# MLP block products: hi and lo of the right operand in one matmul of 512 columns

## The chip, the cores and the metric

One core of one Trainium2 chip runs the whole kernel. The metric is the device time of one execution in microseconds (us). All five engines of the core work at once, each through its own queue in a fixed order: TensorE (PE) multiplies, VectorE (DVE) and ScalarE (ACT) do elementwise work, GpSimd (POOL) a few small operations, and the Sync engine's queue (SP) issues the loads.

## The reference

One block of a streaming encoder, 512 positions of 1024 features, in float32: a first part (input projection, gated branches, output projection), which the change leaves as it is, and then a squared-ReLU MLP with a hidden width of 4096 and a final norm.

```python
hf = rmsnorm(x, norm_ff_g[l])
z = jax.nn.relu(jnp.einsum('bsd,df->bsf', hf, w_ff1[l]))     # 1024 -> 4096
x = x + jnp.einsum('bsf,fd->bsd', z * z, w_ff2[l])            # 4096 -> 1024
return rmsnorm(x, norm_final_g)
```

## The kernel before

Features lie on the partitions, the 512 positions on the columns. To keep float32 accuracy with the faster fp32r matmul, every operand is split into a hi part (a cast, by ACT) and a lo part (operand minus hi, by DVE), `split_into` (L114), and each product is made of three matmuls, hi x hi, hi x lo and lo x hi, that add up in one PSUM bank. There are 7 banks in rotation.

The second MLP layer is made of plain units (`unit_k`, L262): for each of 8 slices of 128 features three matmuls of 512 columns (L265 to L267).

The first layer and some projections use a block scheme with seven instead of eight products. An output pair is 256 hidden features; its weights are four blocks, and what is multiplied is blocks of weights or sums of them (`a1`, `s31`, `s42`, `a22`) with halves of 256 positions or sums of those (the right operands, `right_of`, L322). `product` (L273) makes one of the seven: 4 slices with three matmuls of 256 columns each (L283 to L285). `block_pair` (L289) makes the products of a pair in the order P1, P2, E, P6, F, and puts P7 and D aside (`late`); they run among the next pair's products. Three banks serve a pair: A collects P1, P6, P7 and D, E collects E and F, P2 has its own; only the first 256 columns of each are used. After each product ACT or DVE reads the running sum out of the bank: copies by ACT (L298, L303, L305, L313), adds by DVE (L300, L308, L314).

The results go through `z_first` and `z_second` (L718, L722): max or min with zero and the factor 1/rms (R) on DVE, a square on ACT, and the split into z's hi (ACT) and lo (DVE), 128x512 each.

Weights come in loads of 1 MB with two load buffers (`raw`). `plan_pair` (L207) lists the steps that prepare a pair's weights: hi and lo of a1, a weight sum (L218), hi and lo of s31, two more sums (L222, L223), hi and lo of s42, hi and lo of a22. All lo parts and sums are DVE's. `pump` (L180) takes one step per product from that list if one of four buffers is free, so the preparation of later products stands in the same DVE and ACT queues as the reading of the banks.

The MLP runs in four passes (L844): 5, 4, 4 and 3 pairs of the first layer, each followed by eight units of the second layer on the eight z tiles made. Within each engine the final order is set by a scheduler when the program is built: it reorders instructions by its own estimate of when they can start, and may put matmuls of different products between one another. That order is fixed afterwards; on the chip an engine waits at each instruction for what it needs.

Of the kernel before, what the change touches and what calls it, by code (L numbers as in the profile page):

```python
# [12 lines left out]
ALU = mybir.AluOpType  # L13
# [23 lines left out]
def hybrid_block(ctx, tc, xT, vecs, w_v, w_main, w_pair, w_s, b_s, out_a, out_b):  # L37
# [12 lines left out]
    nc = tc.nc  # L50
# [46 lines left out]
    def slots(n, name, dtype=F32):  # L97
        return [Slot(f"{name}{k}", dtype) for k in range(n)]
# [8 lines left out]
    def temp(name, n=S):  # L107
        t = work.tile([P, S + 2], F32, tag="temp", name=name)
        return t[:, :n]

    def col(base, j):
        return vec[:, base + j : base + j + 1]

    def split_into(hi, lo, src, scale=None):  # L114

        if scale is None:
            nc.scalar.copy(hi, src)  # L117
            nc.vector.tensor_tensor(lo, src, hi.bitcast(F32), op=ALU.subtract)  # L118
# [55 lines left out]
    def release(o):  # L174
        if o["n"] == 2:
            wfree.append(o["buf"])
        else:
            a22_busy[0] = False

    def pump(n=1):  # L180

        while steps and n:
            step, o = steps[0]
            if o is not None and (not wfree if o["n"] == 2 else a22_busy[0]):
                return
# [50 lines left out]
    late = []  # L236

    def run_late():
        if late:
            late.pop(0)()  # L240
# [7 lines left out]
    def unit_matmuls(psum, act_hi, act_lo):  # L248

        o = units[state["next"]]  # L250
        state["next"] += 1
        for k in range(KT):
            if k == 0 or k == KT // 2:
                pump()
                need(o)
            unit_k(psum, o, k, act_hi, act_lo)
            if k == KT // 2 - 1:
                run_late()
        release(o)
        run_late()  # L260
# [9 lines left out]
    LEFT = {"P1": ("a1", 1, "B11"), "P2": ("a1", 0, "B21"), "D": ("a22", 0, "T4"), "F": ("s42", 0, "B22"),  # L270
            "P6": ("s42", 1, "T2"), "E": ("s31", 1, "T1"), "P7": ("s31", 0, "T3")}

    def product(p, right, name, out, first):  # L273

        t, g, r = LEFT[name]
        o = pairs[p][t]
        pump()
        need(o)
        for sl in range(KS):
            c = slice(sl * P, (sl + 1) * P)  # L280
            w_hi, w_lo = o["hi"][:, g, c], o["lo"][:, g, c]
            x_hi, x_lo = right[r, sl, 0], right[r, sl, 1]
            nc.tensor.matmul(out, w_hi, x_hi, start=first and sl == 0, stop=False, skip_group_check=True)  # L283
            nc.tensor.matmul(out, w_hi, x_lo, start=False, stop=False, skip_group_check=True)  # L284
            nc.tensor.matmul(out, w_lo, x_hi, start=False, stop=sl == KS - 1, skip_group_check=True)  # L285
        if name in ("P2", "D", "F", "P7"):
            release(o)

    def block_pair(p, right, first, second):  # L289

        A, P2, E = (bank()[:, :N2] for _ in range(3))
        c1, c2 = temp("c1"), temp("c2")
        product(p, right, "P1", A, True)
        nc.scalar.copy(c1[:, :N2], A)  # L298
        product(p, right, "P2", P2, True)
        nc.vector.tensor_add(c1[:, :N2], P2, c1[:, :N2])  # L300
        run_late()
        product(p, right, "E", E, True)
        nc.scalar.copy(c2[:, N2:], E)  # L303
        product(p, right, "P6", A, False)
        nc.scalar.copy(c1[:, N2:], A)  # L305
        run_late()
        product(p, right, "F", E, False)
        nc.vector.tensor_add(c1[:, N2:], E, c1[:, N2:])  # L308
        first(c1)

        def p7():
            product(p, right, "P7", A, False)
            nc.scalar.copy(c2[:, :N2], A)  # L313
            nc.vector.tensor_add(c2[:, N2:], c2[:, :N2], c2[:, N2:])  # L314

        def dd():
            product(p, right, "D", A, False)
            second(A, c2)

        late.extend([p7, dd])  # L320

    def right_of(b11, b2, t1, t2):  # L322

        r = {}
        for sl in range(KS):
            for hl in range(2):
                r["B11", sl, hl] = b11(sl, hl)
                for ss, two in ((b2, ("B21", "B22")), (t1, ("T1", "T3")), (t2, ("T2", "T4"))):
                    for e in range(2):
                        r[two[e], sl, hl] = ss[sl].t[:, hl, e * N2 : (e + 1) * N2]  # L330
        return r

    def combos(t1, t2, xa, xb):

        B11, B12, B21, B22 = xa[:, :N2], xa[:, N2:], xb[:, :N2], xb[:, N2:]
        a, b = temp("T1T3"), temp("T2T4")
        nc.vector.tensor_sub(a[:, :N2], B11, B12)
        nc.vector.tensor_sub(a[:, N2:], B22, B12)
        nc.vector.scalar_tensor_tensor(b[:, :N2], a[:, :N2], -1.0, B22, op0=ALU.mult, op1=ALU.subtract)
        nc.vector.scalar_tensor_tensor(b[:, N2:], b[:, :N2], -1.0, B21, op0=ALU.mult, op1=ALU.subtract)  # L340
        split_into(t1.t[:, 0, :], t1.t[:, 1, :], a)
        split_into(t2.t[:, 0, :], t2.t[:, 1, :], b)
# [11 lines left out]
    def rstd_of(acc, lo=0, n=NB):  # L354

        st = ps1.tile([P, S], F32, name="st")
        for b in range(n):
            nc.tensor.matmul(  # L358
                st[:, b : b + 1], acc[:, lo + b * P : lo + (b + 1) * P], inv_d, start=True, stop=True
            )  # L360
        return rstd_cols(st[:, :n])
# [32 lines left out]
    n_win = len(pairs)  # L394
# [8 lines left out]
    x_s = slots(KT, "x", F32R)  # L403
# [45 lines left out]
    xc1, xc2 = [], []  # L449
# [10 lines left out]
    r = None  # L460
# [3 lines left out]
    for i in range(2 * KT):  # L464
# [4 lines left out]
        if i == KT:  # L469
            r = rstd_of(acc)  # L470
# [4 lines left out]
        for ws, xs in ((vh, xh), (vl, xh), (vh, xl)):  # L475
            for b in range(NB):
                nc.tensor.matmul(  # L477
                    vbanks[h][b], xs[k][:, b * P : (b + 1) * P], ws,
                    start=k == 0 and ws is vh and xs is xh, stop=k == KT - 1 and xs is xl,
# [62 lines left out]
    for j in range(KT):  # L542
# [6 lines left out]
            mix(j - LAG)  # L549

    right_x = right_of(
        lambda sl, hl: x_s[sl].t[:, hl, :N2], x_s[KS:], xc1, xc2
    )

    def gate(p, n, j0, then):
# [124 lines left out]
    fb11 = slots(KS // 2, "fb11", F32R)  # L680
# [1 line left out]
    ft1 = slots(KS, "ft1", F32R)  # L682
    ft2 = slots(KS, "ft2", F32R)

    def f_b11(sl, hl):
        return fb11[sl // 2].t[:, hl, (sl % 2) * N2 : (sl % 2 + 1) * N2]

    right_f = right_of(f_b11, fb2, ft1, ft2)
    xg = {}
    for n in range(KT):  # L690
        j = n // 2 + KS * (n % 2)
        po = bank()
        unit_matmuls(po, mh, ml)
        nc.vector.tensor_add(res[j], po, res[j])
        xg[j] = temp("xg")
        nc.scalar.activation(xg[j], res[j], AF.Copy, scale=col(V_GFF, j))
        if n % 2:
            split_into(fb2[j - KS].t[:, 0, :], fb2[j - KS].t[:, 1, :], xg[j])
            combos(ft1[j - KS], ft2[j - KS], xg.pop(j - KS), xg.pop(j))
        else:  # L700
            split_into(f_b11(j, 0), f_b11(j, 1), xg[j][:, :N2])
        sum_squares(acc, res[j], n)
    give(*m_s)

# [2 lines left out]
    Rf = small.tile([P, S], F32, name="R")  # L707
# [6 lines left out]
    def z_split(i, t):  # L714
        nc.scalar.activation(t, t, AF.Square)
        split_into(*z_tile(i), t)

    def z_first(i, c1):  # L718
        nc.vector.scalar_tensor_tensor(c1, c1, 0.0, Rf, op0=ALU.max, op1=ALU.mult)
        z_split(i, c1)  # L720

    def z_second(i, n21, c2):  # L722

        nc.vector.scalar_tensor_tensor(c2[:, :N2], n21, 0.0, Rf[:, :N2], op0=ALU.min, op1=ALU.mult)
        nc.vector.scalar_tensor_tensor(c2[:, N2:], c2[:, N2:], 0.0, Rf[:, N2:], op0=ALU.min, op1=ALU.mult)
        z_split(i, c2)

    def scale_g(j, cs):
# [75 lines left out]
    def ff1_pair(p):  # L804
        def first(c1):
            if p == 0:
                wait_rf.append(lambda: z_first(0, c1))
            else:
                z_first(2 * p, c1)

        def second(n21, c2):
            z_second(2 * p + 1, n21, c2)

        block_pair(n_win + p, right_f, first, second)
        if p == 0:
            r2.append(rstd_of(acc))

            def p7_and_rf(p7=late.pop(0)):
                p7()
                nc.vector.tensor_copy(Rf, spread(r2[0]))  # L820
                wait_rf.pop()()
            late.insert(0, p7_and_rf)
# [112 lines left out]
```

## Time and profile before

| what | us |
|---|---|
| median of 3 runs | 788.54 |
| the profiled execution | 788.42 |
| its span in the trace | 786.6 |
| PE busy in it | 778.4 |
| DVE busy | 568.8 |
| ACT busy | 365.7 |

A span is the time from the first to the last instruction of the trace. Busy is the time in which an engine works on at least one instruction; matmuls overlap, so that a busy PE says nothing on how closely they follow one another. In a timeline each row has a start and a duration; the distance of two starts is what one instruction costs an engine that is never idle. "<-" behind an idle time names what ended it. The trace puts the output projection ahead of 440 us, the first pass's block products at 440 to 496, and the second layer's units behind each pass.

### The profile page before, as it was taken

What the parts mean: (1) busy time and instruction counts of PE and PEld (TensorE: products, weight loads), DVE (VectorE), ACT (ScalarE), POOL (GpSimd) and SP (SyncE); (2) the same over time, 40 slices, a digit from 0 to 9 for tenths busy, and PEclk for the clock granted to TensorE, in tenths of its full rate; (3) what the DMA queues carried; (4) which work ended last, traced back from release to release, by engine and by line L of the source; (5) the groups of instructions that cost most, each with busy time, mean ns of one, the idle gap of its engine ahead of it and who ended that gap; (6) DMA issues with size and microseconds to landing.
All of it is one profiled execution on the core that took longest, in us unless ns stands there. A gap on an engine that the chain in (4) does not pass through costs nothing.

```text
span 786.6 us, 11560 instructions
## 1 busy us (share of the span) xinstructions
PE 778.4 (99%) x4798; PEld 701.3 (89%) x4798; DVE 568.8 (72%) x854; ACT 365.7 (46%) x548; POOL 6.3 (1%) x14
## 2 busy tenths in 40 slices
PE   9999999999999999999999999999999999999996
PEld 6888899999999999999988999889988999889886
DVE  7849785566889889766769998647955687557644
ACT  8625363444344444444555676324742365226521
POOL 0000000000000000000000000000000000000000
PEclk9999999999999999999999999999999999999998
DMA  9602113331332314332633033330353024311403
GB/s 333 218 40 92 68 55 107 107 107 55 107 115 102 107 62 154 107 108 86 229 114 107 1 107 125 144 107 1 107 182 140 1 91 177 107 54 55 161 1 107
DMA packets 21443, 83.60 MB, mean 106 GB/s; under 512 B 1936, under 2 KB 2960, under 8 KB 17296
## 3 DMA queue, kind: packets, MB, share of 16 engines
q1 hardware_dynamic: 20384, 81.27, 29.5%
q10 hardware_dynamic: 1008, 1.61, 0.6%
q8 instruction: 37, 0.61, 0.3%
q14 instruction: 14, 0.11, 0.0%
HBM read 80.78 MB, written 2.10 MB: 105 GB/s over the span
## 4 chain that ended last, share of the span: by engine, by line
PE 98%; DMA 0%; ACT 0%; DVE 0%; POOLq 0%; DVEq 0%; issue 0%
PE bank L265 17%; PE bank L266 17%; PE bank L267 17%; PE bank L284 14%; PE bank L285 14%; PE bank L283 14%; PE bank L477 6%; PE bank L528 1%; DMA vec<-vecs 0%; PE bank L369 0%; PE st L358 0%; PE bank L747 0%; PE st L793 0%; DVE ob L759 0%; POOLq L929 0%; ACT x L120 0%
## 5 line engine op out<-in xcount | busy, mean ns | idle before, releaser
L117 ACT CAST whi<-raw 128x1024 fp32r<-128x1024 f32 (+1 forms) x136 | 129.0, 950 | 180.4 <-PE bank L266 117.7
L118 DVE TENSOR_TENSOR wlo<-raw,whi 128x1024 fp32r<-128x1024 f32 (+1 forms) x136 | 148.8, 1096 | 18.2 <-ACT whi L117 16.3
L117 ACT CAST whi<-wsum 128x1024 fp32r<-128x1024 f32 x64 | 67.2, 1051 | 80.9 <-PE bank L266 41.3
L265 PE MATMUL bank<-z,whi 128*128 128x512 f32 (+1 forms) x272 | 102.7, 378 | 0.0
L266 PE MATMUL bank<-z,whi 128*128 128x512 f32 (+1 forms) x272 | 102.6, 377 | 0.0
L267 PE MATMUL bank<-z,wlo 128*128 128x512 f32 (+1 forms) x272 | 102.4, 376 | 0.0
L118 DVE TENSOR_TENSOR wlo<-wsum,whi 128x1024 fp32r<-128x1024 f32 x64 | 78.2, 1222 | 21.0 <-ACT whi L117 20.2
L283 PE MATMUL bank<-ft,whi 128*128 128x256 f32 x256 | 72.5, 283 | 0.0
L285 PE MATMUL bank<-xc,wlo 128*128 128x256 f32 x256 | 72.4, 283 | 0.0
L284 PE MATMUL bank<-xc,whi 128*128 128x256 f32 x256 | 72.4, 283 | 0.0
L285 PE MATMUL bank<-ft,wlo 128*128 128x256 f32 x256 | 72.4, 283 | 0.0
L284 PE MATMUL bank<-ft,whi 128*128 128x256 f32 x256 | 72.4, 283 | 0.0
L283 PE MATMUL bank<-xc,whi 128*128 128x256 f32 x256 | 72.3, 282 | 0.0
L860 DVE TENSOR_TENSOR res<-bank,res 128x512 f32<-128x512 f32 x30 | 20.7, 691 | 60.9 <-PE bank L267 60.9
L267 PEld LDWEIGHTS bank<-z,wlo 128*128 128x128 f32 x272 | 51.2, 188 | 9.4
L265 PEld LDWEIGHTS bank<-z,whi 128*128 128x128 f32 x272 | 51.2, 188 | 9.2
L266 PEld LDWEIGHTS bank<-z,whi 128*128 128x128 f32 x272 | 51.2, 188 | 8.9
L284 PE MATMUL bank<-fb,whi 128*128 128x256 f32 x192 | 54.4, 283 | 0.0
L283 PE MATMUL bank<-fb,whi 128*128 128x256 f32 x192 | 54.4, 283 | 0.0
L283 PE MATMUL bank<-x,whi 128*128 128x256 f32 x192 | 54.4, 283 | 0.0
L285 PE MATMUL bank<-x,wlo 128*128 128x256 f32 x192 | 54.3, 283 | 0.0
L284 PE MATMUL bank<-x,whi 128*128 128x256 f32 x192 | 54.3, 283 | 0.0
(157 smaller groups left out, 1797.6 us busy)
## 6 DMA issues: line engine op xcount, KB each, us to landing
raw<-w_main SPq DMA_DIRECT2D x36, 1024.0 KB, 4.9
raw<-w_pair SPq DMA_DIRECT2D x32, 1024.0 KB, 4.8
vraw<-w_v SPq DMA_DIRECT2D x16, 256.0 KB, 5.5
xin<-xT SPq DMA_DIRECT2D x8, 256.0 KB, 5.2
res<-xT SPq DMA_DIRECT2D x8, 256.0 KB, 4.7
out_a<-o SPq DMA_DIRECT2D x4, 256.0 KB, 2.3
wsT<-w_sT ACTq DMA_DIRECT2D x2, 256.0 KB, 4.8
bsb<-b_sb ACTq DMA_DIRECT2D x2, 256.0 KB, 6.0
```

Source lines behind the costliest of these rows:

```text
L117: nc.scalar.copy(hi, src)
L118: nc.vector.tensor_tensor(lo, src, hi.bitcast(F32), op=ALU.subtract)
L265: nc.tensor.matmul(psum, hi[:, c], act_hi[k][:, cols], start=k == 0, stop=False)
L266: nc.tensor.matmul(psum, hi[:, c], act_lo[k][:, cols], start=False, stop=False)
L267: nc.tensor.matmul(psum, lo[:, c], act_hi[k][:, cols], start=False, stop=k == KT - 1)
L283: nc.tensor.matmul(out, w_hi, x_hi, start=first and sl == 0, stop=False, skip_group_check=True)
L284: nc.tensor.matmul(out, w_hi, x_lo, start=False, stop=False, skip_group_check=True)
L285: nc.tensor.matmul(out, w_lo, x_hi, start=False, stop=sl == KS - 1, skip_group_check=True)
L477: nc.tensor.matmul(vbanks[h][b], xs[k][:, b * P : (b + 1) * P], ws, start=k == 0 and ws is vh and xs is xh, stop=k == KT - 1 and xs is xl,)
L528: nc.tensor.matmul(pm[:, b * P : (b + 1) * P], vt[b][g // 4][:, (g % 4) * P : (g % 4 + 1) * P], wsT[:, g, :], start=True, stop=True,)
L860: nc.vector.tensor_add(res[j], py, res[j])
```

## The change

In the MLP's first layer (16 pairs) a slice's first two matmuls, hi x hi and hi x lo, become one: the right operand's hi and lo, two runs of 256 columns, are read as one moving operand of 512 columns and land in the two halves of the bank. The third, lo x hi, still adds 256 columns to the first half. The halves are added when the bank is read: the copies and adds take all 512 columns, and a further add on DVE (`fold`) sums the halves. For D, ACT copies the second half and DVE adds it to the first. `z_second` gets its result in one piece. The block products of the first part keep their form. The file's later lines move: `product` is at L273 in both, its matmuls at L291 (512) and L295 (256), and the new function's at L333.

```diff
+    def product(p, right, name, out, first, wide=False):
+        half, two = out[:, :N2], out.rearrange("p (e n) -> p e n", e=2)
...
+            x2 = right[r, sl]
+            x_hi, x_lo = x2[:, 0, :], x2[:, 1, :]
+            if wide:
+                nc.tensor.matmul(two, w_hi, x2, start=first and sl == 0, stop=False, **kw)
+            else:
+                nc.tensor.matmul(half, w_hi, x_hi, start=first and sl == 0, stop=False, **kw)
+                nc.tensor.matmul(half, w_hi, x_lo, start=False, stop=False, **kw)
+            nc.tensor.matmul(half, w_lo, x_hi, start=False, stop=sl == KS - 1, **kw)
...
+    def wide_pair(p, right, first, second):
+        A, P2, E = (bank() for _ in range(3))
+        c1, c2 = temp("c1"), temp("c2")
+        t1, t2, t3 = temp("t1"), temp("t2"), temp("t3")
+        def fold(out, t):
+            nc.vector.tensor_add(out, t[:, :N2], t[:, N2:])
+        product(p, right, "P1", A, True, wide=True)
+        nc.scalar.copy(t1, A)
+        product(p, right, "P2", P2, True, wide=True)
+        nc.vector.tensor_add(t1, P2, t1)
+        fold(c1[:, :N2], t1)
+        run_late()
+        product(p, right, "E", E, True, wide=True)
+        nc.scalar.copy(t2, E)
+        product(p, right, "P6", A, False, wide=True)
+        nc.scalar.copy(t3, A)
+        run_late()
+        product(p, right, "F", E, False, wide=True)
+        nc.vector.tensor_add(t3, E, t3)
+        fold(c1[:, N2:], t3)
+        first(c1)
+        def p7():
+            product(p, right, "P7", A, False, wide=True)
+            t4 = temp("t4")
+            nc.scalar.copy(t4, A)
+            nc.vector.tensor_add(t2, t4, t2)
+            fold(c2[:, N2:], t2)
+        def dd():
+            product(p, right, "D", A, False, wide=True)
+            t5 = temp("t5", N2)
+            nc.scalar.copy(t5, A[:, N2:])
+            nc.vector.tensor_add(c2[:, :N2], A[:, :N2], t5)
+            second(c2)
...
-        nc.vector.scalar_tensor_tensor(c2[:, :N2], n21, 0.0, Rf[:, :N2], op0=ALU.min, op1=ALU.mult)
-        nc.vector.scalar_tensor_tensor(c2[:, N2:], c2[:, N2:], 0.0, Rf[:, N2:], op0=ALU.min, op1=ALU.mult)
+        nc.vector.scalar_tensor_tensor(c2, c2, 0.0, Rf, op0=ALU.min, op1=ALU.mult)
...
-        block_pair(n_win + p, right_f, first, second)
+        wide_pair(n_win + p, right_f, first, second)
```

The scheduler's order on DVE, first pass, around the add of the fourth pair's P2. Before (c1_4473 is that pair's first result, wlo_4542 the lo of its s42, wlo_4604 and wlo_4635 the lo of the fifth pair's a1 and s31):

```order
L118 TENSOR_TENSOR wlo_4542<-wsum1_104,whi_4541 128x1024
L300 TENSOR_TENSOR c1_4473<-bank_4471,c1_4473 128x256
L118 TENSOR_TENSOR z4_4118<-c1_4347,z4_4118 128x512
L314 TENSOR_TENSOR c2_4348<-c2_4348 128x256
L725 SCALAR_TENSOR_TENSOR c2_4348<-c2_4348,R_4113 128x256
L218 TENSOR_TENSOR wsum0_103<-raw_4475 128x1024
L118 TENSOR_TENSOR wlo_4604<-raw_4475,whi_4603 128x1024
L222 TENSOR_TENSOR wsum1_104<-wsum0_103,raw_4475 128x512
L118 TENSOR_TENSOR wlo_4635<-wsum0_103,whi_4634 128x1024
```

After (t1_4422 is the sum that the fourth pair's P2 goes into, wlo_4479 the lo of its s42, wlo_4535 the lo of the fifth pair's a1):

```order
L345 TENSOR_TENSOR t1_4422<-bank_4418,t1_4422 128x512
...
L340 TENSOR_TENSOR c1_4420<-t1_4422 128x256
L222 TENSOR_TENSOR wsum1_104<-wsum0_103,raw_4318 128x512
L118 TENSOR_TENSOR wlo_4535<-raw_4425,whi_4534 128x1024
L118 TENSOR_TENSOR z4_4118<-c1_4313,z4_4118 128x512
L362 TENSOR_TENSOR t2_4316<-t4_4463,t2_4316 128x512
L223 TENSOR_TENSOR wsum1_104<-wsum1_104,raw_4318 128x512
L340 TENSOR_TENSOR c2_4314<-t2_4316 128x256
L118 TENSOR_TENSOR wlo_4507<-raw_4318,whi_4506 128x512
L218 TENSOR_TENSOR wsum0_103<-raw_4425 128x1024
L118 TENSOR_TENSOR wlo_4479<-wsum1_104,whi_4478 128x1024
```

The lo of s42, which P6 and F of the same pair need, has moved from just ahead of the add to twelve rows behind it, and the row of P2 is followed by a fold further down.

PE's order at the fourth pair's P6. Before (bank_4470 is the pair's A, whi_4541 and wlo_4542 its s42):

```order
L283 MATMUL bank_4470<-ft20_3762,whi_4541 128x256
L284 MATMUL bank_4470<-ft20_3762,whi_4541 128x256
L285 MATMUL bank_4470<-ft20_3762,wlo_4542 128x256
L283 MATMUL bank_4470<-ft21_3763,whi_4541 128x256
L284 MATMUL bank_4470<-ft21_3763,whi_4541 128x256
```

After (bank_4417 is A, bank_4419 is E, whi_4478 and wlo_4479 the pair's s42; bank_4526 is the fifth pair's E bank, whi_4558 the hi of its s31):

```order
L291 MATMUL bank_4417<-ft20_3762,whi_4478 128x512
L291 MATMUL bank_4419<-fb20_3754,whi_4478 128x512
L291 MATMUL bank_4526<-ft10_3758,whi_4558 128x512
L295 MATMUL bank_4417<-ft20_3762,wlo_4479 128x256
L291 MATMUL bank_4417<-ft21_3763,whi_4478 128x512
L295 MATMUL bank_4417<-ft21_3763,wlo_4479 128x256
```

Three products now begin with one wide matmul each, among them the fifth pair's E, before the first matmul that needs s42's lo.

## Rows read from the trace of the kernel before

**Rows 1.** The page's part 1: busy us, share of the span, instructions, by engine.

```profile
PE 778.4 (99%) x4798; PEld 701.3 (89%) x4798; DVE 568.8 (72%) x854; ACT 365.7 (46%) x548; POOL 6.3 (1%) x14
```

**Rows 2.** The page's part 4: shares of the span in the chain that ended last.

```profile
PE 98%; DMA 0%; ACT 0%; DVE 0%; POOLq 0%; DVEq 0%; issue 0%
```

**Rows 3.** Timeline of PE, block products: start us, us, engine, line, operation, tiles.

```profile
455.18 0.28 PE L285 MATMUL bank<-ft,wlo 128*128 128x256 f32 x1
...
456.98 0.28 PE L285 MATMUL bank<-fb,wlo 128*128 128x256 f32 x1
```

**Rows 4.** Timeline of PE, second-layer units, same columns.

```profile
510.00 0.39 PE L265 MATMUL bank<-z,whi 128*128 128x512 f32 x1
...
514.99 0.39 PE L266 MATMUL bank<-z,whi 128*128 128x512 f32 x1
```

**Rows 5.** Stretches: length, then busy us (instructions) per engine, granted clock, DMA share, GB/s.

```profile
430.00:440.00 10.00, 10.00 (x54) 8.63 (x53) 9.86 (x17) 5.82 (x9) 0.00 (x0) 1.00 0.00 0
440.00:450.00 10.00, 10.00 (x85) 9.98 (x85) 9.03 (x18) 6.20 (x11) 1.91 (x1) 1.00 0.01 2
450.00:460.00 10.00, 10.00 (x87) 10.00 (x86) 9.81 (x17) 7.28 (x14) 0.00 (x0) 1.00 0.13 37
500.00:510.00 10.00, 10.00 (x45) 8.26 (x44) 4.95 (x6) 2.73 (x3) 0.00 (x0) 1.00 0.28 105
620.00:630.00 10.00, 10.00 (x86) 10.00 (x85) 7.64 (x10) 6.02 (x9) 0.00 (x0) 1.00 0.01 2
640.00:650.00 10.00, 10.00 (x86) 10.00 (x85) 9.31 (x15) 7.33 (x12) 0.00 (x0) 1.00 0.30 105
780.00:790.00 10.00, 0.14 (x2) 0.00 (x0) 1.47 (x3) 1.27 (x2) 0.69 (x1) 0.68 0.29 105
```

**Rows 6.** Timeline of DVE, one pair of the first MLP pass.

```profile
470.17 1.23 DVE L118 TENSOR_TENSOR wlo<-wsum,whi 128x1024 fp32r<-128x1024 f32 x1 [0.18 <-ACT whi L117]
471.31 0.42 DVE L300 TENSOR_TENSOR c<-bank,c 128x256 f32<-128x256 f32 x1
471.65 0.68 DVE L118 TENSOR_TENSOR z<-c,z 128x512 fp32r<-128x512 f32 x1
472.25 0.42 DVE L314 TENSOR_TENSOR c<-c 128x256 f32<-128x256 f32 x1
472.70 0.42 DVE L725 SCALAR_TENSOR_TENSOR c<-c,R 128x256 f32<-128x256 f32 x1
...
480.25 1.23 DVE L118 TENSOR_TENSOR wlo<-wsum,whi 128x1024 fp32r<-128x1024 f32 x1
```

**Rows 7.** Groups by line and form: xcount | busy us, mean ns | idle before.

```profile
L860 DVE TENSOR_TENSOR res<-bank,res 128x512 f32<-128x512 f32 x30 | 20.7, 691 | 60.9 <-PE bank L267 60.9
...
L298 ACT COPY c<-bank 128x256 f32<-128x256 f32 x32 | 11.9, 371 | 13.5 <-PE bank L285 13.3
...
L440 ACT ACTIVATE vt<-bank,r 128x512 f32<-128x512 f32 x8 | 4.9, 689 | 10.8 <-PE bank L477 9.5 <-POOL r L351 1.4
```

**Rows 8.** Timeline, start and end of the first MLP pass's block products (PE and DVE).

```profile
443.65 0.36 PE L283 MATMUL bank<-fb,whi 128*128 128x256 f32 x1
...
443.81 0.42 DVE L300 TENSOR_TENSOR c<-bank,c 128x256 f32<-128x256 f32 x1
...
495.58 0.28 PE L285 MATMUL bank<-ft,wlo 128*128 128x256 f32 x1
495.70 0.40 PE L265 MATMUL bank<-z,whi 128*128 128x512 f32 x1
```

**Rows 9.** Timeline of ACT, first MLP pass: square, cast, hi part, copy.

```profile
459.11 0.63 ACT L715 ACTIVATE c<-c 128x512 f32<-128x512 f32 x1
459.78 0.62 ACT L117 CAST z<-c 128x512 fp32r<-128x512 f32 x1
...
462.45 1.05 ACT L117 CAST whi<-raw 128x1024 fp32r<-128x1024 f32 x1 [0.46 <-DMA raw<-w_pair]
463.40 0.37 ACT L303 COPY c<-bank 128x256 f32<-128x256 f32 x1
```

More of the change, by code (lines that the diff above doesn't have):

```diff
@@ L271, in hybrid_block @@
             "P6": ("s42", 1, "T2"), "E": ("s31", 1, "T1"), "P7": ("s31", 0, "T3")}
-    def product(p, right, name, out, first):
+    def product(p, right, name, out, first, wide=False):
+        half, two = out[:, :N2], out.rearrange("p (e n) -> p e n", e=2)
         t, g, r = LEFT[name]
@@ L281, in product @@
             w_hi, w_lo = o["hi"][:, g, c], o["lo"][:, g, c]
[L282 to L285, printed above, removed]
+            x2 = right[r, sl]
+            x_hi, x_lo = x2[:, 0, :], x2[:, 1, :]
+            kw = dict(skip_group_check=True)
+            if wide:
[4 more added lines that the diff above has]
+            nc.tensor.matmul(half, w_lo, x_hi, start=False, stop=sl == KS - 1, **kw)
         if name in ("P2", "D", "F", "P7"):
@@ L289, in block_pair @@
     def block_pair(p, right, first, second):
-        A, P2, E = (bank()[:, :N2] for _ in range(3))
+        A, P2, E = (bank() for _ in range(3))
+        A_, P2_, E_ = (b[:, :N2] for b in (A, P2, E))
         c1, c2 = temp("c1"), temp("c2")
         product(p, right, "P1", A, True)
-        nc.scalar.copy(c1[:, :N2], A)
+        nc.scalar.copy(c1[:, :N2], A_)
         product(p, right, "P2", P2, True)
-        nc.vector.tensor_add(c1[:, :N2], P2, c1[:, :N2])
+        nc.vector.tensor_add(c1[:, :N2], P2_, c1[:, :N2])
         run_late()
         product(p, right, "E", E, True)
-        nc.scalar.copy(c2[:, N2:], E)
+        nc.scalar.copy(c2[:, N2:], E_)
         product(p, right, "P6", A, False)
-        nc.scalar.copy(c1[:, N2:], A)
+        nc.scalar.copy(c1[:, N2:], A_)
         run_late()
         product(p, right, "F", E, False)
-        nc.vector.tensor_add(c1[:, N2:], E, c1[:, N2:])
+        nc.vector.tensor_add(c1[:, N2:], E_, c1[:, N2:])
         first(c1)
@@ L312, in p7 @@
             product(p, right, "P7", A, False)
-            nc.scalar.copy(c2[:, :N2], A)
+            nc.scalar.copy(c2[:, :N2], A_)
             nc.vector.tensor_add(c2[:, N2:], c2[:, :N2], c2[:, N2:])
@@ L317, in dd @@
             product(p, right, "D", A, False)
-            second(A, c2)
+            second(A_, c2)
+        late.extend([p7, dd])
+    def wide_pair(p, right, first, second):
+        A, P2, E = (bank() for _ in range(3))
+        c1, c2 = temp("c1"), temp("c2")
[29 more added lines that the diff above has]
+            second(c2)
         late.extend([p7, dd])
@@ L325, in right_of @@
         for sl in range(KS):
[L326 to L330, printed above, removed]
+            r["B11", sl] = b11(sl)
+            for ss, two in ((b2, ("B21", "B22")), (t1, ("T1", "T3")), (t2, ("T2", "T4"))):
+                for e in range(2):
+                    r[two[e], sl] = ss[sl].t[:, :, e * N2 : (e + 1) * N2]
         return r
@@ L551, in hybrid_block @@
     right_x = right_of(
-        lambda sl, hl: x_s[sl].t[:, hl, :N2], x_s[KS:], xc1, xc2
+        lambda sl: x_s[sl].t[:, :, :N2], x_s[KS:], xc1, xc2
     )
@@ L683, in hybrid_block, with f_b11 @@
     ft2 = slots(KS, "ft2", F32R)
-    def f_b11(sl, hl):
-        return fb11[sl // 2].t[:, hl, (sl % 2) * N2 : (sl % 2 + 1) * N2]
+    def f_b11(sl):
+        return fb11[sl // 2].t[:, :, (sl % 2) * N2 : (sl % 2 + 1) * N2]
     right_f = right_of(f_b11, fb2, ft1, ft2)
@@ L700, in hybrid_block @@
         else:
-            split_into(f_b11(j, 0), f_b11(j, 1), xg[j][:, :N2])
+            split_into(f_b11(j)[:, 0, :], f_b11(j)[:, 1, :], xg[j][:, :N2])
         sum_squares(acc, res[j], n)
@@ L720, in z_first, with z_second @@
         z_split(i, c1)
-    def z_second(i, n21, c2):
-        nc.vector.scalar_tensor_tensor(c2[:, :N2], n21, 0.0, Rf[:, :N2], op0=ALU.min, op1=ALU.mult)
-        nc.vector.scalar_tensor_tensor(c2[:, N2:], c2[:, N2:], 0.0, Rf[:, N2:], op0=ALU.min, op1=ALU.mult)
+    def z_second(i, c2):
+        nc.vector.scalar_tensor_tensor(c2, c2, 0.0, Rf, op0=ALU.min, op1=ALU.mult)
         z_split(i, c2)
@@ L809, in first, with second @@
                 z_first(2 * p, c1)
-        def second(n21, c2):
-            z_second(2 * p + 1, n21, c2)
-        block_pair(n_win + p, right_f, first, second)
+        def second(c2):
+            z_second(2 * p + 1, c2)
+        wide_pair(n_win + p, right_f, first, second)
         if p == 0:
```

## The prediction

> **What bounds the kernel now.** I read the busy shares first: TensorE (PE) is busy 778.4 us, 99% of the span of 786.6, VectorE (DVE) 568.8, 72% [rows 1]. The chain that ended last is 98% PE, with next to nothing given to a wait [rows 2]. So TensorE's own stream of matmuls sets the time, and only what shortens that stream or makes it wait can move it. "Busy" does not say how dense the stream is, so I took start-to-start distances from the timeline. In the block products 256 columns come every 0.120 us (15 steps from 455.18 to 456.98) [rows 3]; in the plain units 512 columns come every 0.2268 us (22 steps from 510.00 to 514.99) [rows 4]. Two matmuls of 256 thus take 0.240, one of 512 takes 0.227: a matmul has some 13 ns that do not depend on its columns, and that is all a merged pair gives back. The granted clock is 1.00 in the stretches shown up to 650, so these are figures at 2.4 GHz [rows 5].
>
> Then the stretches of 10 us show who stands second [rows 5]. In the first MLP pass DVE is busy 9.03 to 9.81 us of each 10 while the block products run; in later passes' products 7.64 to 9.31; in the second-layer units (500 to 510) only 4.95. ScalarE (ACT) is at 6.0 to 7.3. The reader should see that DVE has almost no room exactly where the change gives it more work.
>
> **What the change removes.** 16 MLP pairs x 7 products x 4 slices = 448 slices, each with one matmul less: 448 x (2 x 0.120 - 0.2268) = 5.9 us of PE. PE per pair falls from 28 x 0.36 = 10.08 to 28 x 0.3468 = 9.71 us. The weight load that goes with the removed matmul is off the path: a load overlaps the matmul ahead of it: PE goes on at the same steps in the units, where loads are busy 8.26 of 10 us, as in products, where they are busy 10.00 [rows 5].
>
> No row shows a matmul whose moving operand is two runs of 256 columns. The bounds: as one run, 0.2268 [rows 4]; as two matmuls, 0.240 [rows 3]. I take 0.2268, since columns and output bank are those of rows 4; the other end costs the whole 5.9 us.
>
> The Trainium skill, "TensorE: Matmul & The Clock Gate", section "Back-to-back issue gap", gives a gap of N/2.4 + 2.5 ns, and speaks against the change: by it a merged pair saves 2.5 ns, all of them 1.1 us. The trace has 120 and 227 ns where that gives 109 and 216, so the measurement decides.
>
> **What it adds on DVE.** Starts behind one another in the timeline: 128x1024 takes 1.14 (470.17 to 471.31), 128x256 0.34 (471.31 to 471.65), 128x512 0.60 (471.65 to 472.25); one that needs the row ahead of it 0.45 rather than 0.34 (472.25 to 472.70) [rows 6]. An add that reads a bank is no dearer: of 512 it lasts 691 ns, as the others in the timeline (0.68 to 0.69) [rows 6, 7]. Before, a pair has 4 of 1024 (three lo splits and one weight sum), 6 of 512 and 5 of 256: 9.86 us, and the trace repeats after 10.08 (470.17 to 480.25) [rows 6]. After, the adds of P2, F and P7 are 512 wide, there are three folds and D's add of 256, and the two half mins are one of 512: 4, 10 and 4, or 11.92 us. That is 2.06 us more, up to 2.4 with the dependent neighbours; 33 to 38 us for 16 pairs.
>
> **What it adds on ACT.** Four copies per pair grow from 256 columns (371 ns) to 512 (at most the 689 ns of the GELU that reads a bank), and one copy of 256 is new: at most 4 x 0.32 + 0.37 = 1.65 us per pair, and by a SBUF cast of 512 (620 ns) 4 x 0.25 + 0.37 = 1.4 [rows 7, 9]. ACT has that room, 2.7 us or more in 10 [rows 5]; it counts only where DVE or PE waits for it.
>
> So per pair DVE needs 12.0 to 12.3 us against PE's 9.7, a deficit of about 2.5. It falls on PE only when the operands' lo parts, which stand in the same DVE queue, come late. Bounds: nothing, if the lead in prepared weights holds (-5.9 us in all); everything (38 - 5.9 = +32 us). I narrow this by walking the two orders with those durations.
>
> **First pass (5 pairs).** DVE has no lead here: it comes from the output projection busy 9.86 of 10 us [rows 5]. DVE's order is unchanged up to the add of the first P2, at 443.81 [rows 8], so I start there, with PE at the product that it resumes at 443.65 [rows 8]. A product is 4 x 0.3468 = 1.39 us, one without its first matmul 1.16.
> 1. The spread of 1/rms. The last of its four scales now stands on DVE behind s42's lo of pair two. ACT can begin the hi parts ahead of it when P2 of pair two has let a buffer go, at 448.7; it makes two (0.95 each, start to next start [rows 9], and handing over) until 450.9, DVE adds 1.14 for the lo, 0.35 for a fold and 0.25 for the scale: 452.75. PE has 37 matmuls (6.4), one product and the small matmuls (0.6) until 452.05. Wait 0.8 us.
> 2. Pair four's a1. DVE's next 15 rows (2 of 1024, 10 of 512, 3 of 256: 9.3, and 0.3 for dependent neighbours) end at 462.3; behind them ACT has a square (0.67), a cast (some 0.55) and then a1's hi of 0.95 to 1.05 [rows 9]: 464.65. PE, seven products (9.7) on from 452.85, is there at 462.55. Wait 2.1.
> 3. s31's hi and s42's lo in the next group of products: 0.5.
> 4. In the before order s42's lo stands ahead of P2's add; now it stands 12 rows behind, and the first matmul of E waits for s31's hi, which waits for the weight sum on DVE. For pair five's E PE is there at 479.5; the sum is done at 480.4, the hi at 481.5. Wait 2.0.
> 5. s42's lo of pair five at 488.65, PE at 487.75: 0.9.
>
> The waits are 6.3 us. From 488.65 PE still has four products, 22 matmuls of 512 (5.0) and the rest of a product: the fifth D ends at 500.4, and two of its second-layer matmuls (0.45) are ones that before stood behind the fifth D. Without them that is 499.9 against 495.70 [rows 8]: +4.2 us, the waits less the saving.
>
> **Passes two to four (4, 4 and 3 pairs).** In the units ahead of them DVE is half idle [rows 5], so each begins with a pair's weights split ahead. The same walk over four pairs gives DVE 37.6 us for its rows up to the last s42, and PE waits of 0.2 (E's bank, still being copied) and 1.8 us (first second-layer unit's lo), against 1.5 saved: +0.5 each. With three pairs some 1.0 against 1.1: -0.1. The backlog left over drains in the units that follow, where DVE needs under 6 of 10 us.
>
> **Sum.** 4.2 + 0.5 + 0.5 - 0.1 = +5.1 us. The profiled execution took 788.42 with a span of 786.6; 788.42 + 5.1 = 793.5. The median of the runs is 788.54, the same within 0.02%.
>
> **Rivals.**
> - *All hidden.* Later passes leave DVE 1 to 2 us free in 10 [rows 5], and PE waits nowhere today [rows 2]. Time: 788.4 - 5.9 = 782.5. Against it: the first pass has no such room.
> - *DVE pays in full (slower).* If every pair runs at DVE's pace, 16 x 2.4 - 5.9 = +32: 820.5. It decides (over 804.3) once about 22 of the 38 us land on PE, that is nine pairs of sixteen. For it: waits between three queues feed one another, and my walk grants each the shortest. Against it: passes two to four start with a lead and end in units with slack. The Trainium skill's "Trainium Kernel Development and Optimization", "Best Practices", says that tiling on TensorE speeds up compute but not PSUM evacuation; here the reading of the banks even grows, and rows 6 carry the price.
> - *No saving in the merged matmul.* Two runs cost 0.240: 793.5 + 5.9 = 799.4.
> - *The clock falls in the waits.* PE's granted clock is 0.68 only in the last stretch, where PE does almost nothing [rows 5]. If waits of 1 to 2 us had that effect, 50 us of products at 1.2 GHz would add 50: 843. No wait in this trace shows it.
>
> **Chances.** Forecast 0.62; all hidden 0.12; no saving 0.10; DVE in full 0.10; clock 0.03; something else 0.03. Within 2% (772.8 to 804.3, about what a measurement of this kernel tells from no change) lie the first three: 0.85 with a share of the last. Slower: 0.14. Faster needs more than the whole 5.9 us: 0.01. The range runs from all hidden, 782, to where DVE's full price begins to decide, 804.
>
> **What would show it.** 448 fewer matmuls; pairs of 0.227 and 0.120 in dense stretches (step one). DVE at 9.5 or more of 10 us through the first pass's products, and PE gaps there of 1 to 2 us whose releasers are ACT's whi or DVE's wlo, 6 us in all. In later passes at most one gap of 1 to 2 us, near the first second-layer unit. A wide matmul at 0.240, gaps in every pair, or a granted clock below 1.00 in 440 to 500 would each prove me wrong.

## The result, and the profile after

The changed kernel takes 795.77 us (median of 4 runs; the profiled execution 795.82, its span 793.7), the kernel before 788.5 (median of 4). The ratio of the means is 1.0104, 95% interval 1.0059 to 1.015: about 1% slower, inside the 2% that counts as no change. By the median that is 2.3 us above the forecast of 793.5 and inside its range. One of the four runs of the kernel before took 1293.41 us and is left out of the ratio; one of the changed kernel's took 800.19 and is in it.

The page of the kernel after, its part 1 (busy us, share of the span, instructions by engine) and the first line of its part 4 (shares in the chain that ended last), which answer [rows 1, 2]:

```profile
PE 779.6 (98%) x4350; PEld 677.2 (85%) x4350; DVE 600.3 (76%) x902; ACT 379.5 (48%) x564; POOL 6.2 (1%) x14
...
PE 92%; DVE 4%; ACT 1%; DMA 1%; issue 0%; POOLq 0%; DVEq 0%; ACTq 0%
```

There are 448 matmuls fewer, as there should be. DVE has 31.5 us more work. PE's share of the chain fell from 98 to 92%: other engines now stand on the path. Which ones is told by the view of waits of PE in the kernel after (what waited, for what; us in all, how often, the longest):

```profile
PE bank L291 <- ACT whi L117: 2.7, 2, 1.4
PE bank L267 <- DVE wlo L118: 1.8, 2, 1.3
PE bank L265 <- ACT whi L117: 1.7, 2, 1.3
PE st L78 <- DVE warm L65: 1.0, 1, 1.0
```

The last row is at the start of the kernel and is in every kernel's list. The other three are new. Three of their six waits lie in the first pass. The timeline of PE in the kernel after shows them (the time in brackets is the idle time before the row, with what ended it):

```profile
462.65 0.28 PE L295 MATMUL bank<-ft,wlo 128*128 128x256 f32 x1
464.30 0.73 PE L291 MATMUL bank<-fb,whi 128*128 128x512 f32 x2 [1.37 <-ACT whi L117]
...
479.61 0.40 PE L291 MATMUL bank<-fb,whi 128*128 128x512 f32 x1
481.34 0.50 PE L291 MATMUL bank<-ft,whi 128*128 128x512 f32 x1 [1.33 <-ACT whi L117]
...
487.82 0.50 PE L265 MATMUL bank<-z,whi 128*128 128x512 f32 x1 [0.36 <-ACT whi L117]
488.15 0.40 PE L266 MATMUL bank<-z,whi 128*128 128x512 f32 x1
488.63 0.39 PE L295 MATMUL bank<-ft,wlo 128*128 128x256 f32 x1
```

ACT is named, but it is only the last link. For the wait that ends at 481.34, ACT's and DVE's timelines of the kernel after show who was late:

```profile
480.24 1.04 ACT L117 CAST whi<-wsum 128x1024 fp32r<-128x1024 f32 x1 [1.02 <-DVE wsum L218]
```

```profile
478.38 0.69 DVE L118 TENSOR_TENSOR wlo<-raw,whi 128x512 fp32r<-128x512 f32 x1
478.99 1.22 DVE L218 TENSOR_TENSOR wsum<-raw 128x1024 f32<-128x1024 f32 x1
480.12 2.42 DVE L118 TENSOR_TENSOR wlo<-wsum,whi 128x1024 fp32r<-128x1024 f32 x2
```

ACT had itself waited 1.02 us for the weight sum, and DVE reached that sum only at 478.99, with work queued on both sides. The windows of the kernel after, columns as in [rows 5], show DVE full there and PE below ten, all at full clock:

```profile
450.00:460.00 10.00, 10.00 (x61) 8.73 (x60) 9.90 (x17) 5.96 (x12) 0.00 (x0) 1.00 0.08 13
460.00:470.00 10.00, 8.63 (x46) 6.81 (x46) 10.00 (x15) 7.09 (x11) 0.00 (x0) 1.00 0.33 109
470.00:480.00 10.00, 9.86 (x55) 7.88 (x53) 9.74 (x17) 6.47 (x10) 0.00 (x0) 1.00 0.22 91
480.00:490.00 10.00, 8.23 (x44) 6.55 (x44) 9.76 (x16) 7.99 (x13) 0.00 (x0) 1.00 0.31 105
```

Passes two and three have waits near the first second-layer unit, pass two one and pass three two (PE, kernel after):

```profile
572.80 0.40 PE L266 MATMUL bank<-z,whi 128*128 128x512 f32 x1
574.47 0.51 PE L267 MATMUL bank<-z,wlo 128*128 128x512 f32 x1 [1.27 <-DVE wlo L118]
...
658.72 0.50 PE L265 MATMUL bank<-z,whi 128*128 128x512 f32 x1 [1.35 <-ACT whi L117]
...
659.97 0.51 PE L267 MATMUL bank<-z,wlo 128*128 128x512 f32 x1 [0.53 <-DVE wlo L118]
```

To see what each pass costs I took, in every kernel's trace, the start of DVE's add of the pass's last second-layer unit, the row with the line of [rows 7]'s first group (534.00 in the first pass before, 538.36 after), and the distance from one pass's to the next. The first column is against the kernel before and also holds the first part's end, which moves by 0.0 to 0.6 us between these kernels (1.0 in e9); the others are the differences of the distances. The kernels e1 to e12 come below.

| kernel | to end of pass 1 | pass 2 | pass 3 | pass 4 |
|---|---|---|---|---|
| before, us | 534.00 | 83.90 | 83.90 | 62.93 |
| after | +4.36 | +1.31 | +1.83 | -0.47 |
| e1 added work alone | +5.41 | +1.15 | +1.14 | +0.06 |
| e2 merge alone | -0.35 | -0.73 | -0.73 | -0.61 |
| e4 pass 1 narrow | 0.00 | +1.22 | +1.36 | -0.32 |
| e9 before, sum on POOL | +4.63 | +0.46 | +0.47 | 0.00 |
| e10 grouped | +4.98 | -0.51 | -0.26 | -0.71 |
| e11 grouped, pass 1 narrow | +0.55 | -0.49 | -0.49 | -0.66 |
| e12 grouped, pass 4 alone | +0.44 | 0.00 | 0.00 | +0.08 |

### The profile page after: what moved, and what is told of

It reads as the page before. It is cut to its first block, busy times and chain, and to the rows that moved or that the text cites. A ratio compares the mean times of both kernels' runs of the same rounds, so it can differ in the third digit from the quotient of the medians.

```text
span 793.7 us, 10751 instructions
## 1 busy us (share of the span) xinstructions
PE 779.6 (98%) x4350; PEld 677.2 (85%) x4350; DVE 600.3 (76%) x902; ACT 379.5 (48%) x564; POOL 6.2 (1%) x14
## 4 chain that ended last, share of the span: by engine, by line
PE 92%; DVE 4%; ACT 1%; DMA 1%; issue 0%; POOLq 0%; DVEq 0%; ACTq 0%
PE bank L267 17%; PE bank L265 16%; PE bank L266 16%; PE bank L295 12%; PE bank L291 10%; PE bank L294 7%; PE bank L293 7%; PE bank L528 6%; DVE wlo L118 1%; PE bank L579 1%; DMA raw<-w_main 1%; ACT whi L117 1%; DVE c L340 0%; DVE z L118 0%; DMA vec<-vecs 0%
## 5 line engine op out<-in xcount | busy, mean ns | idle before, releaser
L291 PE MATMUL bank<-ft,whi 128*128 128x512 f32 x256 | 92.8, 401 | 1.5 <-ACT whi L117 1.3
L295 PE MATMUL bank<-xc,wlo 128*128 128x256 f32 x256 | 72.6, 284 | 0.0
L295 PE MATMUL bank<-ft,wlo 128*128 128x256 f32 x256 | 71.8, 282 | 0.1
L291 PE MATMUL bank<-fb,whi 128*128 128x512 f32 x192 | 68.6, 399 | 1.4 <-ACT whi L117 1.4
L291 PEld LDWEIGHTS bank<-ft,whi 128*128 128x128 f32 x256 | 48.1, 188 | 14.6 <-ACT whi L117 2.9
L295 PE MATMUL bank<-x,wlo 128*128 128x256 f32 x192 | 54.4, 284 | 0.0
L295 PE MATMUL bank<-fb,wlo 128*128 128x256 f32 x192 | 52.5, 281 | 0.0
```

The source lines that it names most:

```text
L291: nc.tensor.matmul(two, w_hi, x2, start=first and sl == 0, stop=False, **kw)
L295: nc.tensor.matmul(half, w_lo, x_hi, start=False, stop=sl == KS - 1, **kw)
```

## The experiments

### What the merge alone saves, and what the added work alone costs

**e1** keeps the new reading of the banks and undoes the merge: two matmuls of 256 into the two halves.

```diff
-                nc.tensor.matmul(two, w_hi, x2, start=first and sl == 0, stop=False, **kw)
+                nc.tensor.matmul(out[:, :N2], w_hi, x_hi, start=first and sl == 0, stop=False, **kw)
+                nc.tensor.matmul(out[:, N2:], w_hi, x_lo, start=False, stop=False, **kw)
```

> The changed kernel with its wide matmul taken apart again: two matmuls of 256 columns into the two halves of the bank; all that DVE and ACT do stays as changed. Theory A (the merged matmul saves only half of the forecast, 6.5 ns a slice, since a wide and a narrow matmul take 0.3535 us in the changed trace instead of 0.3468; the loss is in waits for DVE and for ACT behind DVE): dense slices at 0.360, about 448 x 6.5 ns = 2.9 us slower than the changed kernel, less what the waits shrink by, so 797 to 799. Theory B (the merge saves the forecast 13 ns a slice): up to 5.9 us slower, 800 to 802.

Measured: 796.07 us against 788.91, ratio 1.0089 (1.0074 to 1.0104). **e2** does the reverse: wide matmuls, but the banks are read as before, the first half alone.

```diff
-        wide_pair(n_win + p, right_f, first, second)
+        block_pair(n_win + p, right_f, first, second_h, wide=True)
```

> The merge without its reading: wide matmuls as changed, but the banks are read as before, the first 256 columns alone (the hi x lo part is left out of the result). DVE and ACT have the work of the kernel before. Theory A: no waits, 448 x 6.5 ns = 2.9 us off, 785.6. Theory B: 5.9 off, 782.6. If DVE's added work were not what makes PE wait, waits of 1 to 2 us would stay and the time would be near 790.

Measured: 785.92, ratio 0.9962 (0.9947 to 0.9977), 3.0 us less, and no wait of PE in the MLP. So the added work alone, DVE's and ACT's, in the order that the scheduler makes of it, costs 7.2 us, and the merge alone saves 3.0. Both together cost 7.3, not 4.2: with DVE setting the pace, a shorter stream of matmuls for the most part makes PE wait sooner. e1's time was below both of its expectations: the waits without the merge are shorter still than I had allowed.

The 3.0 is half of what I had predicted, and the timeline of PE in e2 shows why (the kernel after has the same steps, 17 slices from 539.91 to 545.92):

```profile
540.50 0.40 PE L291 MATMUL bank<-fb,whi 128*128 128x512 f32 x1
540.74 0.28 PE L295 MATMUL bank<-fb,wlo 128*128 128x256 f32 x1
540.86 0.40 PE L291 MATMUL bank<-fb,whi 128*128 128x512 f32 x1
541.10 0.28 PE L295 MATMUL bank<-fb,wlo 128*128 128x256 f32 x1
541.21 0.40 PE L291 MATMUL bank<-fb,whi 128*128 128x512 f32 x1
541.45 0.28 PE L295 MATMUL bank<-fb,wlo 128*128 128x256 f32 x1
541.56 0.40 PE L291 MATMUL bank<-fb,whi 128*128 128x512 f32 x1
```

Three slices take 1.06 us, 0.353 each. The median over the whole trace is 0.236 for a wide matmul behind a narrow one and 0.118 for the narrow one between two wide. The saving of a slice is 0.360 - 0.3535 = 6.5 ns; 448 of them are 2.9 us.

**e3** asks whether the second run of the moving operand is to blame: as e2, but each wide matmul reads one run of 512 columns (other numbers, so another result).

```diff
-                nc.tensor.matmul(two, w_hi, x2, start=first and sl == 0, stop=False, **kw)
+                nc.tensor.matmul(two, w_hi, run[r, sl], start=first and sl == 0, stop=False, **kw)
```

> As the kernel with the merge alone, but the wide matmul reads one run of 512 columns (a whole hi row) instead of two runs of 256 that lie 512 apart; the result is another one. Theory C (the missing half of the saving is the second run of the moving operand): a slice at 0.347, 782.6. Theory D (it belongs to changing between 512 and 256 columns, or to the weight loads): a slice at 0.3535, 785.6 as with two runs.

Measured: 786.65, ratio 0.9969 (0.9958 to 0.9979), with the steps of e2, 0.236 and 0.118, and an interval that overlaps that of e2. The second run costs nothing. **e5** asks whether the alternation of widths does it: as e2, with the four wide matmuls of a product first and its four narrow ones behind them.

```diff
+            for sl, w_hi, w_lo, x2, x_hi, x_lo in parts:
+                nc.tensor.matmul(two, w_hi, x2, start=first and sl == 0, stop=False, **kw)
+            for sl, w_hi, w_lo, x2, x_hi, x_lo in parts:
+                nc.tensor.matmul(half, w_lo, x_hi, start=False, stop=sl == KS - 1, **kw)
```

> The kernel with the merge alone (banks read as before, hi x lo left out of the result), with each product's four wide matmuls first and its four narrow ones behind them. Theory E (a wide matmul costs its extra 7 to 9 ns only behind a narrow one): a product falls from 1.414 to about 1.394 us, 112 x 0.020 = 2.2 us less than with the merge alone, 783.7. Theory F (every wide matmul of the MLP costs 0.235): 785.9 as before.

Measured: 785.0, ratio 0.9955 (0.9942 to 0.9969), between the two expectations. PE's timeline in e5:

```profile
541.38 1.09 PE L292 MATMUL bank<-fb,whi 128*128 128x512 f32 x4
542.31 0.64 PE L294 MATMUL bank<-fb,wlo 128*128 128x256 f32 x4
542.79 1.09 PE L292 MATMUL bank<-ft,whi 128*128 128x512 f32 x4
543.72 0.63 PE L294 MATMUL bank<-ft,wlo 128*128 128x256 f32 x4
544.19 1.09 PE L292 MATMUL bank<-ft,whi 128*128 128x512 f32 x4
```

A product takes 1.405 us (two from 541.38 to 544.19), where alternating it takes 1.414 and by 0.227 and 0.120 it would take 1.388. So grouping gets back about a third of what is missing: by the medians, the first two wide matmuls of a group still step 0.234, the third 0.229, and only the fourth 0.227. So the alternation is not all of it, and what makes the first ones slower than the units' 0.227 these runs don't tell.

### Whether the passes are independent

**e4** leaves pass one as it was before the change.

```diff
+        if p < CF // 2 + 1:
+            block_pair(n_win + p, right_f, first, second_h)
+        else:
+            wide_pair(n_win + p, right_f, first, second)
```

> The first MLP pass (5 pairs) in the form of before, the other three passes (11 pairs) wide as changed. By the times at which each pass ends in the two traces the first pass costs 4.1 us, the second 1.3, the third 1.8, the fourth gains 0.5. If the passes are independent of one another: 788.5 + 2.6 = 791.1 (790.5 to 792). If the backlog of the first pass is what makes the later ones wait: at or under 788.

Measured: 791.67, ratio 1.0037 (1.0022 to 1.0051). The waits of PE in e4:

```profile
PE bank L267 <- DVE wlo L118: 2.5, 2, 1.3
PE st L78 <- DVE warm L65: 1.0, 1, 1.0
PE bank L265 <- ACT whi L117: 0.5, 2, 0.2
```

The two waits of up to 1.3 us for a lo, near the first unit of passes two and three, are there without any backlog from pass one. Of the 7.3 us, pass one has about 4.4, and passes two and three 3.1, of which pass four gives back 0.5.

### Taking work off DVE

If DVE is the cause, taking rows from it should bring PE's waits down. **e6** moves the folds to POOL, **e7** the 1024-column weight sum of each MLP pair, **e8** does that with the order of e5.

```diff
-            nc.vector.tensor_add(out, t[:, :N2], t[:, N2:])
+            nc.gpsimd.tensor_add(out, t[:, :N2], t[:, N2:])
```

```diff
+            eng = nc.gpsimd if no >= 2 * KT else nc.vector
-            nc.vector.tensor_tensor(s31, raw(1, 3), raw(3, 4).broadcast_to([P, 2, S]), op=ALU.add)
+            eng.tensor_tensor(s31, raw(1, 3), raw(3, 4).broadcast_to([P, 2, S]), op=ALU.add)
```

> The changed kernel with its three folds per pair on POOL instead of DVE. They are 1.0 to 1.3 us of DVE's added 2.06 to 2.4 a pair. Theory A (DVE's added work makes PE wait): the waits, some 9 us in all, fall by more than half, 789 to 792. Against it: if POOL's fold is slow, or POOL's work slows DVE's, the first results come later and the time stays or rises, 796 or more.

> The changed kernel with the weight sum of 128x1024 that s31's hi waits for on POOL instead of DVE, in the MLP's 16 pairs. It is 1.14 us of DVE per pair, and in the trace the two longest waits of the first pass stand behind it or behind work queued with it. Theory A: the wait ahead of the fifth pair's E (1.5 us at 481.3) goes, and those of later passes with it: 787 to 790. Against it: POOL may need several us for the sum; above 5 us s31 would come late in each pair and the time exceed 796.

> The changed kernel with the weight sum on POOL and each product's wide matmuls ahead of its narrow ones. With theory E some 2 us under the kernel with the sum on POOL, 785 to 788, if PE's waits do not take it up; in that order the lo parts are needed later in a product, which shortens waits for them by up to 0.7 us each. With theory F as that kernel or a little less.

Measured: 801.04 (ratio 1.0155, 1.0139 to 1.017), 804.59 (1.0201, 1.0184 to 1.0218) and 797.14 (1.0112, 1.0096 to 1.0127). They are 9, 15 and 9 us above the upper ends of what relief for DVE should have given. In e7 DVE's busy time is 599.5 us, where 16 sums of 1.22 should have left it at 581. POOL's and DVE's timelines in e7 show where they went:

```profile
465.77 3.29 POOL L220 TENSOR_TENSOR wsum<-raw 128x1024 f32<-128x1024 f32 x1 [14.90 <-DMA raw<-w_pair]
477.18 2.55 POOL L220 TENSOR_TENSOR wsum<-raw 128x1024 f32<-128x1024 f32 x1 [8.12 <-DMA raw<-w_pair]
...
549.44 2.40 POOL L220 TENSOR_TENSOR wsum<-raw 128x1024 f32<-128x1024 f32 x1 [11.52 <-DVE wlo L118]
```

```profile
466.85 3.29 DVE L118 TENSOR_TENSOR wlo<-wsum,whi 128x1024 fp32r<-128x1024 f32 x1
...
477.61 2.69 DVE L118 TENSOR_TENSOR z<-c,z 128x512 fp32r<-128x512 f32 x1 [0.15 <-ACT z L117]
...
551.32 0.69 DVE L356 TENSOR_TENSOR t<-bank,t 128x512 f32<-128x512 f32 x1 [1.96 <-PE bank L297]
```

DVE's lo of 1024, elsewhere 1.22 us, takes 3.29: POOL's sum ends at 469.06, the lo at 470.14, about its own length later. The lo of z, elsewhere 0.69, takes 2.69 and ends 0.57 us behind POOL's second sum. So an operation of DVE with two inputs in SBUF that begins within one of POOL's gets nowhere until POOL is done: in e7 and e9 each one of 512 columns that began so ends 0.55 to 0.56 us behind the sum. The add that reads a bank (551.32, while the sum runs until 551.84) takes its usual 0.69. POOL waits in the same way. The first sum is itself longer than the second; it began while DVE was at two operations that end at 466.81, and it ends 2.25 us behind them, about what the third sum takes in all. The Trainium skill, "Advanced Engine Details and Errata", section "GPSIMD Details", says that POOL shares a read and a write interface with DVE and conflicts with DVE instructions that have two SBUF inputs; these rows agree.

**e9** is the control: the same sum on POOL in the kernel before the change.

> The kernel before the change with the 1024-column weight sum of each MLP pair on POOL: the control of the run that did this to the changed kernel. Theory S (POOL's 2.6 us per sum and the longer DVE operations beside it are what cost there, whatever DVE's load): here too DVE's busy time does not fall, by under 5 of the 19.5 us taken off it, and waits appear: 792 or more. Theory N (they cost only because DVE was already full): 788.5 to 789.5, no PE gap over 0.5 us.

Measured: 795.02, ratio 1.0083 (1.0066 to 1.01). Theory S: POOL costs 6.3 us also without the change, and DVE's busy time falls by 4.7 us of the 19.5 taken off it. By the table most of the cost (4.6 us) has come by the end of pass one, the pass in which DVE is nearly full before [rows 5]; passes two and three pay 0.5 each. POOL's group and a DVE group in e9 (687 ns in the kernel before), and the first row of the waits of PE in e9:

```profile
L220 POOL TENSOR_TENSOR wsum<-raw 128x1024 f32<-128x1024 f32 x16 | 41.1, 2566 | 617.3 <-DMA raw<-w_pair 483.0 <-DVE wlo L118 91.2 <-ACT c L315 28.9
...
L118 DVE TENSOR_TENSOR wlo<-raw,whi 128x512 fp32r<-128x512 f32 x32 | 28.3, 886 | 0.8
```

```profile
PE bank L285 <- ACT c L305: 2.4, 3, 2.0
```

So e6 to e8 say nothing on the price of DVE's load: what they took off it, POOL took back. That the added work in DVE's queue is the cause rests on e1, e2 and the rows of the kernel after. e1 has ACT's longer copies and the scheduler's new order in it as well; no run takes these apart.

### The order within a product

e8 was 7.5 us under e7, and the two differ in the order of a product's matmuls alone. **e10** is the changed kernel with that order (the edit of e5) and nothing on POOL.

> The changed kernel, with a product's four matmuls of 512 columns first and its four of 256 behind them; nothing else. Theory G (the price is the waits for hi parts and weight sums, which the order within a product hardly touches): PE's steps shrink by 112 products x 11 ns = 1.2 us (1.414 to 1.403 us each), the small waits for lo parts (0.5 and 0.25 us in pass one) go, the two of 1.5 us for ACT's hi stay: about 793.5 to 794.5. Theory L (most of the waits hang on when the first lo part is needed, now 0.7 us later in every product, as the 7.5 us between the two kernels with the sum on POOL suggest): 787 to 790, and gaps of PE in pass one under 2 us in all.

Measured: 791.58, ratio 1.0037 (1.0024 to 1.005), 4.2 us less than the changed kernel, between the two theories. The waits of PE in e10, and the longest in its timeline:

```profile
PE bank L292 <- ACT whi L117: 3.3, 3, 1.7
PE st L78 <- DVE warm L65: 1.0, 1, 1.0
PE bank L292 <- ACT t L353: 0.9, 2, 0.6
```

```profile
485.40 1.21 PE L292 MATMUL bank<-ft,whi 128*128 128x512 f32 x4 [1.69 <-ACT whi L117]
```

Theory G holds for pass one: the two long waits for ACT's hi stay (1.41 and 1.69 us, where the changed kernel has 1.37 and 1.33, and one of 0.19). Theory L holds for passes two and three: the waits for a lo near the first unit are gone, and these passes now gain 0.5 and 0.3 us (table). By the table the gain comes from passes two to four (4.15 us in all); pass one ends 0.6 us later than in the changed kernel. In the new order PE has a product and more between the first unit's second and third matmul (573.59 and 576.72 in e10's trace), so that the third, which needs the lo, comes later. The order within a product changed the scheduler's order around it; I did not separate these two. The windows of e10 show that DVE is no less full in pass two than in the changed kernel (9.82 and 9.18 us there, PE 10.00 and 8.59):

```profile
560.00:570.00 10.00, 10.00 (x59) 8.75 (x58) 10.00 (x17) 7.50 (x13) 0.00 (x0) 1.00 0.19 66
570.00:580.00 10.00, 9.69 (x53) 8.14 (x52) 10.00 (x18) 7.22 (x12) 0.00 (x0) 1.00 0.42 144
```

So in pass two a full DVE alone does not make PE wait that long: the order decides too. In pass one, where DVE has no lead, the price is there in each of three orders: 4.1 us in the changed kernel, 4.4 in e10, 5.4 in e1 without the merge, all counted from the end of the first part.

**e11** combines e4 and e10: pass one as before the change, passes two to four wide and grouped. **e12** is wide and grouped in pass four alone.

```diff
-        if p < CF // 2 + 1:
+        if p < 13:
```

> Pass one as before the change, passes two to four with wide products in grouped order. Without grouping this was 791.7 against 789 before. Theory G: 77 products x 11 ns = 0.8 us less, waits for the first second-layer unit's lo (1.44 us in each of passes two and three) unchanged: 790.5 to 791. Theory L: the gaps of 0.39 and 1.44 us go, 787.5 to 789, about the kernel before.

> Wide products in pass four alone (three pairs), in grouped order; the other thirteen pairs as before the change. Pass four was the only one that gained, 0.47 us; grouping adds 21 products x 11 ns = 0.2 us. If passes are independent: 0.6 to 0.8 us under the kernel before of the same batch, 788.1 where that is 788.8. If the gain of pass four came from the state in which pass three left DVE, no difference: 788.8.

Measured: e11 787.2 us against 788.71, ratio 0.9983 (0.9973 to 0.9992); e12 788.79, ratio 0.9998 (0.9989 to 1.0008). e11 is the one version with the whole result that beats the kernel before, by 1.5 us (0.2%), and it went below the bounds of both theories. What is left of the waits of PE in it:

```profile
PE st L78 <- DVE warm L65: 1.0, 1, 1.0
PE bank L292 <- ACT t L353: 0.6, 2, 0.3
```

e12 gained nothing, against my expectation of 0.6 to 0.8. Its pass four has a wait that e11's has not, in PE's timeline of e12:

```profile
740.61 0.51 PE L265 MATMUL bank<-z,whi 128*128 128x512 f32 x1
741.34 0.51 PE L266 MATMUL bank<-z,whi 128*128 128x512 f32 x1 [0.22 <-DVE z L118]
```

The two steps into and behind the first row (740.61 is 0.40 behind the row ahead of it, then 0.73) are together 0.67 us longer than two of 0.227, about the 0.66 that pass four gained in e11.

## Why the prediction was right, and where it was off

The forecast, 793.5 and within 2%, held, with the mechanism that it named: DVE, full in the first pass, makes PE wait for hi and lo parts. Two terms were mis-sized, the saving and the waits, and in part they cancelled: that the sum came so near is partly luck.

- **The saving.** Predicted 5.9 us, measured 2.9 (6.5 ns a slice; e2 gives 3.0 by the runs). The step that failed is "I take 0.2268, since columns and output bank are those of rows 4": a matmul's step was taken from a stream of its own width, and put between narrow ones it takes 0.236 (e2; grouped in e5, 0.234 to 0.227). The rival "no saving" was half true, for a reason other than the one given: one run is no faster than two (e3). The trace of before held a hint that I did not use: in it, a unit's 512 columns behind a narrow matmul step 0.233 by the median.
- **DVE's and ACT's added work.** Predicted 33 to 38 us of DVE, measured 31.5 of busy time. ACT's copy of 512 columns lasts 0.58 us (the group of L343 in the kernel after), below the bound of 0.62 to 0.69; ACT's busy time grew by 13.8 us, where 1.4 to 1.65 a pair would be 22 to 26.
- **The first pass, in places.** Hi of pair four's a1: predicted ready at 464.65, PE went on at 464.30. Pair five's s31: predicted 481.5, found 481.34. s42's lo: predicted 488.65, found 488.63. So a walk through two orders with durations from the trace came within 0.35 us over 45 us of full queue. Since the first P2's add itself came 0.30 later than I had it, the walk was 0.3 to 0.65 us too slow.
- **The first pass, in waits.** Predicted 6.3 us, found 4.6: 1.5, 1.5, about 0.8 around 488, and 0.8 in small pieces. PE came later than I had it, since it began later and its slices were longer than I had them, and part of each wait was thereby spent working. The wait for the spread of 1/rms (0.8) is absent: I had PE there at 452.05 and DVE at 452.75; DVE was done at 452.49, and PE issued those matmuls at 452.55 without a gap.
- **The first pass, net.** Predicted +4.2 (its own terms, 6.3 less 1.85 for 140 slices, make 4.45). Found +4.36 at its end, 0.30 of it from ahead of it ([rows 8]: the first P2's add starts 0.30 later), so +4.06. Right, but by two errors of opposite sign, which is luck.
- **Later passes.** Predicted +0.5, +0.5, -0.1, found +1.31, +1.83, -0.47. The wait near the first unit was named and nearly right in pass two (0.2 and 1.8 us predicted, 1.85 in all found); pass three has 2.4. Against it stood half the saving. Most of the 2.3 us by which the forecast was low is here.
- **The sum.** Waits of 8.9 us (4.6, 1.85, 2.4 and none) less 2.9 give +6.0, 0.3 more from ahead of the MLP; the spans differ by 7.0. The remaining 0.7 lies in steps too short to list, among them the step right behind a wait, some 0.11 us longer than elsewhere (487.82 to 488.15: 0.33 rather than 0.227).
- **The rivals.** "All hidden" fell, as PE waited. "DVE pays in full" fell: three quarters of DVE's added work are still hidden (in e1 7.2 us of some 30 show). "The clock falls" fell: it is 1.00 in each window shown, with waits of up to 1.5 us.

The Trainium skill's rule on the back-to-back gap ("TensorE: Matmul & The Clock Gate", "Back-to-back issue gap"), which the page gives for a single matmul by itself, put the saving at 2.5 ns a slice, 1.1 us by an estimate from it; I set 13.2 ns against it, and the runs show 6.5, between the two.

## What to carry to other kernels

Take a matmul's step from rows in which it stands between the neighbours that it will have; a step from a stream of equal widths was off here by 9 ns of 227, and half the gain went with it. Price the stage that the change loads more (the reading of the banks) before the one that it relieves, and in the stretch where that stage is already full: 3 us saved on the first engine were swallowed by 7 us lost through the second. Where some stages have slack and others don't, use the change only where there is slack, and look at the order too: e11 does both and gains 1.5 us, while e4, the same passes without the grouped order, loses 2.8.

## What the runs showed of the hardware

- One run of 512 columns and two runs of 256 as moving operand cost the same (0.236 us behind a narrow matmul, e2 and e3).
- 512 columns step 0.236 us between matmuls of 256 and 0.227 in a stream of their own width; in groups of four behind narrow ones 0.234, 0.234, 0.229, 0.227 (e5).
- POOL's adds in float32 took 0.73 us at least and 1.14 on average for 128x256 (e6), 2.38 at least and 2.57 to 2.62 on average for 128x1024 (e7 to e9), against 0.42 and 1.22 on DVE; the averages hold waits for DVE. An operation of DVE with two SBUF inputs that begins within one lasts until it is over and some (3.29 us rather than 1.22); one with an input in a bank does not (0.69, e7). Work moved to POOL was not off DVE here.
